# Pinning ScalarE's joinings, seeding an accumulator bank by a copy, and moving one residual update into the last block

## The chip, the cores and the metric

The kernel runs on one core of a Trainium2 chip. The core has TensorE (PE in the profile, with PEld for its weight loads), VectorE (DVE), ScalarE (ACT), GpSimd (POOL) and SyncE (SP), which issues most DMAs. The metric is the device time of one execution in microseconds (us).

## The reference, cut to what matters

One decoder layer on 256 tokens of width 2048, in float32: a half-step SwiGLU feed-forward network (FFN, inner width 5632), a mixer (input projection, a recurrent and a convolutional branch, output projection), a second FFN, and a final norm.

```
def swiglu_ffn(x, w_gate, w_up, w_down):
    return (jax.nn.silu(x @ w_gate) * (x @ w_up)) @ w_down
...
x = x + 0.5 * swiglu_ffn(rms_norm(x, ffn1_norm), w_gate1, w_up1, w_down1)
...                       # mixer: x = x + y @ w_out
x = x + 0.5 * swiglu_ffn(rms_norm(x, ffn2_norm), w_gate2, w_up2, w_down2)
return rms_norm(x, final_norm)
```

## The kernel before, in words

**Precision.** Every float32 operand of a product is split into a rounded part `hi` and a remainder `lo`, and a product is three matmuls (hi by hi, lo by hi, hi by lo). For the weights ScalarE makes `hi` by a copy (two halves of 128x1024 each, CAST in the profile), VectorE makes `lo` by a subtraction over 128x2048 (`parts_of`). A weight unit is 512 rows by 512 columns.

**The FFN.** Gate and up projections run column pair by column pair: `for s in range(5)`, each with one call of `seven` for gate and one for up; the first 512 columns are made ahead of this by `begin` or `begin_after`. After s = 0, 2 and 4 a call of `down` multiplies the hidden units made so far by `w_down`; it, too, has one `seven` in it. That makes 13 blocks per FFN and 26 in all.

**A block (`seven`).** Part of each block is a 2x2 block product done with seven products instead of eight (Winograd's form), the rest is usual products over further row units. It has four banks of PSUM, `a`, `c`, `e`, `d`. The order of PE's work is: product 0 into `a`; product 4 into `c`; usual product 0 into `e` and `c`; product 5 into `a`; usual 1 into `e` and `c`; product 6 into `a`; product 2 into `c`; usual 0 into `d` and `a`; product 3 into `a`; usual 1 into `a` and `d`; product 1 into `d`. A product is 12 matmuls, a usual product 24, so a block with two usual units is 180 matmuls. Between products VectorE forms combinations of weight units in place (`raw <- raw, raw`). Some partial sums are needed in more than one quadrant; `snap` has ScalarE copy a bank to a buffer in SBUF (`keep`, 13 buffers): `s1` is `a` after product 0, `s5` is `c` after product 4 (usual 0 can only go on accumulating into `c` once this copy is done), `u2` and `u3` later states of `a`. When a quadrant is complete, `done` adds the bank and its list of copies: quadrant (1, 1) is `e` with two copies, (0, 1) is `c` with one, (1, 0) is `a` alone, (0, 0) is `d` with `s1`. In gate and up `done` leads to `total` (VectorE additions), then Silu on ScalarE or the product of up and gate on VectorE; in `down` it leads to `update`, one VectorE operation on the residual `xres` for the bank and one for each copy.

**Turning the hidden tiles.** Each finished 128x512 hidden tile has to be transposed for use as a stationary operand. `part` shuffles its 16-bit halves apart on ScalarE (into a `plane`, two buffers) and issues a transposing DMA; `join` puts the halves together again on ScalarE (the joining, a COPY of 128x1024 16-bit values into a `plane`), and then splits the result into `hi` (ScalarE) and `lo` (VectorE), and where block sums of it are wanted copies it once more. `onward`, called after each multiply that has two targets, joins the tile that is on its way and parts the next. So a block of two usual units has four such points, and the four tiles that an up block leaves are turned during its own last two points and the next block's first three.

**Order.** A planner takes each engine's instructions in program order and may issue a later one ahead when, in its model, it is ready and the engine is free. The finished order is fixed: on the chip an engine works through its list and waits wherever an operand is late. `tc.keep_in_program_order(ins)` gives `ins` one constraint: it stands behind the instruction that was written just before it for the same engine. While `Engine.pinned` is true, every instruction of VectorE, ScalarE and TensorE gets it. Before, that holds in `begin` and from the last column's update at the end of the second FFN.

**The last `down`.** `side` holds banks for columns 0 and 3, which are multiplied directly: column 0 over all units first, then part of column 3, then the rest of column 0 and its `update` of the residual, then the block (columns 1 and 2), then the rest of column 3. In the last `down` `update` also calls `last`, which squares and sums the new residual on ScalarE (`junk_f`), and multiplies the residual by the final gain on VectorE; its first call loads that gain (`fin`) by a DMA issued on ScalarE's queue.

Of the kernel before, what the change touches and what calls it, by code (L numbers as in the profile page):

```python
# [12 lines left out]
U16 = mybir.dt.uint16  # L13
# [8 lines left out]
NT = S // P  # L22
# [27 lines left out]
def hybrid_block(ctx: ExitStack, tc: tile.TileContext, a: dict, out: bass.AP):  # L50
    nc = tc.nc
    Engine.pinned = False
    dve, act, pe = (Engine(tc, e) for e in (nc.vector, nc.scalar, nc.tensor))
# [29 lines left out]
    def bank(name):  # L83
        return psum.tile([P, 512], F32, tag="ps", name=name)

    def f32(ap):
        return ap.bitcast(F32)
# [62 lines left out]
    def big(name):  # L150

        return bigs.tile([P, UK, 2 * S], F32R, tag="big", name=name)
# [41 lines left out]
    def stationary(tile, t):  # L194

        return [(tile[:, j, t * P : (t + 1) * P], tile[:, j, S + t * P : S + (t + 1) * P]) for j in range(UK)]
# [148 lines left out]
    def quad(tile):  # L345
        return tile.rearrange("p (j c) -> p j c", j=UK)

    def seven(w, rows, cols, sf, xs, name, keep, done, between=None, ready=None):


        a, c, e, d = (bank(f"ps_{name}_{n}") for n in "aced")

        def get(u, n, kept=False):
            src = w[u * UK * P : (u + 1) * UK * P, cols[n] : cols[n] + CW]
            return load(src, f"{name}_{u}{n}", kept=kept)

        (r0, r1), two = rows, len(xs) > 1
        w11, first = ready or (get(r0, 0, True), None)
        w12 = get(r0, 1, True)
        b2, w22 = get(xs[0][0], 1), get(r1, 1)  # L360
        b3 = get(xs[1][0], 1) if two else None
        a2, w21 = get(xs[0][0], 0), get(r1, 0)
        a3 = get(xs[1][0], 0) if two else None

        def snap(ps, n):
            s = keep(f"{n}_{name}")
            act.copy(s, ps)
            return s

        def product_of(i, raw, ps, begin=False, end=True, blk=None):  # L370
            multiply([(ps, sf[i], begin, end)], blk or parts_of(raw, f"{name}_p{i}"), True)

        def usual(i, raw, n, *targets):

            blk = parts_of(raw, f"{name}_x{i}{n}")
            multiply([(ps, stationary(xs[i][1], t), b, z) for ps, t, b, z in targets], blk, True)

        product_of(0, w11, a, True, blk=first)
        s1 = snap(a, "s1")
        dve.tensor_tensor(w11, w12, w11, op=ALU.subtract)  # L380
        product_of(4, w11, c, True)
        s5 = snap(c, "s5")
        if between:
            between(0)
        usual(0, b2, 1, (e, 1, True, not two), (c, 0, False, False))
        if between:
            between(1)
        dve.tensor_tensor(w11, w22, w11, op=ALU.subtract)
        product_of(5, w11, a)
        u2 = snap(a, "u2")  # L390
        if between:
            between(2)
        if two:
            usual(1, b3, 1, (e, 1, False, True), (c, 0, False, False))
        dve.tensor_tensor(w12, w22, w12, op=ALU.subtract)
        product_of(6, w12, a)
        u3 = snap(a, "u3")
        done(1, 1, e, [u3, s5])
        product_of(2, w22, c)
        done(0, 1, c, [u2])  # L400
        usual(0, a2, 0, (d, 0, True, False), (a, 1, False, False))
        dve.tensor_tensor(w11, w21, w11, op=ALU.subtract)
        product_of(3, w11, a, end=not two)
        if two:
            usual(1, a3, 0, (a, 1, False, True), (d, 0, False, False))
        done(1, 0, a, [])
        product_of(1, w21, d)
        done(0, 0, d, [s1])

    def ffn(tag, norm, after, opening=False):  # L410
        with (
# [5 lines left out]
            wg, wu, wd = (a[f"ffn{tag}_w_{s}"][0] for s in ("gate", "up", "down"))  # L417
# [10 lines left out]
            mixed, flat = "p (f b) -> p b f", "p (b f) -> p b f"  # L428
# [10 lines left out]
            def join(two, u, t, h, again):  # L439
                if u not in hidden:  # L440
                    hidden[u] = big(f"h{tag}_{u}")
                act.copy(two.bitcast(U16).rearrange(mixed, b=2), h.bitcast(U16).rearrange(flat, b=2))
                two = quad(two)
                hi = hidden[u][:, :, t * P : (t + 1) * P]
                lo = hidden[u][:, :, S + t * P : S + (t + 1) * P]
                act.copy(hi, two)
                dve.tensor_tensor(lo, two, f32(hi), op=ALU.subtract)
                if again:
                    act.copy(quad(h), two)
                    turned[u, t] = quad(h)  # L450
# [13 lines left out]
            def on_the_way():  # L464
                return [*tiles, *(entry[0] for entry in moving)]
# [3 lines left out]
            units, vs, sf, ready = [], {}, {}, []  # L469
# [198 lines left out]
            xs = list(enumerate(units))[2:]  # L668
            turn_of["hold"] = False

            def down(last):
                us = sorted(set(hidden) | {tile[0] for tile in on_the_way()})
                others, (m, n) = us[:-2], us[-2:]
                end = last and tag == 2

                def update(c, t, *parts):
                    xr = xres[:, t, c * CW : (c + 1) * CW]
                    for p in parts:
                        dve.scalar_tensor_tensor(xr, p, 0.5, xr, op0=ALU.mult, op1=ALU.add)
                    if last:  # L680
                        after(c, t)

                side = {c: [bank(f"ps_d{tag}_{m}_{c}_{t}") for t in range(NT)] for c in (0, 3)}

                def add_units(c, units):
                    blks = [
                        (u, unit(wd[u * UK * P : (u + 1) * UK * P, c * CW : (c + 1) * CW], f"d{tag}_{m}_{c}_{u}"))
                        for u in units
                    ]
                    assert not {tile[0] for tile in on_the_way()} & set(units)  # L690
                    groups = [[0], [1]] if end and units == [n, m] else [[0, 1]]
                    for ts in groups:
                        for u, blk in blks:
                            multiply(
                                [(side[c][t], stationary(hidden[u], t), u == us[0], u == m) for t in ts], blk
                            )
                            pump(1.5 / len(groups))
                    if units[-1] == m:
                        Engine.pinned = end and c == 3
                        for t in range(NT):  # L700
                            update(c, t, side[c][t])

                sh, got, rest = {}, {}, []

                def block_sums():
                    return seven_of(
                        sh, hidden[m], hidden[n],
                        {(t, i): turned[u, t] for t in range(NT) for i, u in ((0, m), (1, n))},
                        quad(keep(f"hspare{tag}_{m}")),
                        [[quad(keep(f"hs{tag}_{m}_{i}_{z}", F32R)) for z in range(2)] for i in range(4)],  # L710
                    )

                def add(t, b, ps, tiles):
                    got[t, b] = [ps] + tiles
                    if (0, b) in got and (1, b) in got:
                        for i in range(NT):
                            update(2 - b, i, *got[i, b])

                for c, u in [(0, u) for u in others + [n]] + [(3, u) for u in others]:
                    add_units(c, [u])  # L720
                    if not on_the_way() and not rest:
                        rest.append(block_sums())
                add_units(0, [m])
                if tag == 1 and m == 5:
                    prepare()
                seven(
                    wd, (m, n), (2 * CW, CW), sh, [(u, hidden[u]) for u in others], f"d{tag}_{m}", keep, add,
                    lambda i: rest.pop()() if rest else None,
                )
                for units in [[n, m]] if end else [[n], [m]]:  # L730
                    add_units(3, units)
                hidden.clear()
                turned.clear()

            for s in range(5):
                cs = (CW + 2 * s * CW, 2 * CW + 2 * s * CW)
# [20 lines left out]
                    if s == 0 and not opening and i != 1:  # L757
                        (sums, lambda: normalise(3))[i // 2]()

                seven(wg, (0, 1), cs, sf, xs, f"g{tag}_{s}", keep, gate, meanwhile, ready.pop() if ready else None)  # L760
                seven(wu, (0, 1), cs, sf, xs, f"u{tag}_{s}", keep, up)
                if s % 2 == 0:
                    down(s == 4)
            extra.clear()
# [45 lines left out]
    with tc.tile_pool(name="mixer", bufs=1) as mp, tc.tile_pool(name="mixw", bufs=2) as mw:  # L810
# [197 lines left out]
        for c in range(NC_D):  # L1008
            cs = slice(c * CW, (c + 1) * CW)
# [96 lines left out]
```

## Time and profile before

| | |
|---|---|
| median of three runs (lowest, highest) | 1740.79 us (1740.5, 1741.35) |
| the profiled execution's own time | 1740.98 us |
| its span, first to last instruction | 1739.2 us |
| mean granted TensorE clock | 0.997 |
| busy: PE, weight loads, DVE, ACT | 1709.3, 1416.1, 1485.4, 1135.1 us |

Nearly all instructions pass through one helper, so their line is 43 and groups are told apart by tile names: `ps_g_a` is bank `a` of a gate block (`u` for up, `d` for down), `hi_g_p` and `lo_g_p` are the parts of a weight unit or combination used in one of the seven products, `hi_g_x` those of a usual product, `plane` the turning buffer. Names like `s_g`, `u_g`, `z`, `s_u` are buffers of `keep` and go on being called by the name under which the tile was made. In a table of windows the number behind x is the count of instructions. The times of matmuls are modelled as pipelined, so a busy PE does not mean a PE at its full rate; counts of matmuls per window show that better.

### The profile page before, as it was taken

How to read it: one execution, taken by the hardware profiler on the slowest of the kernel's cores; microseconds unless marked ns; L12 is line 12 of the kernel's file. 1: busy time of each engine (PE TensorE's matmuls, PEld its weight loads, DVE VectorE, ACT ScalarE, POOL GpSimd, SP SyncE). 2: the span in 40 equal slices, each digit the busy share in tenths (PEclk: the TensorE clock that was granted, in tenths of full speed). 3: DMA queues.
4: the chain of work that ended last, by engine and by line, in shares of the span. 5: the costliest groups of instructions: out<-in, count | busy, mean ns of one | idle time of the engine just before them, and what ended most of it. 6: DMA issues, size and time to landing. Idle time of an engine off the chain costs nothing. (4 is left out here: it accounts for less than half of the span.)

```text
span 1739.2 us, 20156 instructions
## 1 busy us (share of the span) xinstructions
PE 1709.3 (98%) x7859; PEld 1416.1 (81%) x7859; DVE 1485.4 (85%) x1233; ACT 1135.1 (65%) x1433; POOL 6.9 (0%) x32
## 2 busy tenths in 40 slices
PE   8999999999999999999999999999999999999998
PEld 6888787888887888888888888787787888887876
DVE  7997998989899888687986669989799888889786
ACT  6767567676567676665665456675567765676854
POOL 1000000000000000000000000000000000000000
PEclk9999999999999999999999999999999999999999
DMA  8666567594567585556556564595476656576843
GB/s 297 201 218 184 203 215 211 191 303 163 183 217 221 204 247 169 189 172 193 173 194 209 203 217 133 195 289 174 167 235 221 214 173 219 194 212 206 277 167 106
DMA packets 220383, 354.75 MB, mean 204 GB/s; under 512 B 52100, under 2 KB 54528, under 8 KB 220160
## 3 DMA queue, kind: packets, MB, share of 16 engines
q1 hardware_dynamic: 219824, 352.36, 62.5%
q8 instruction: 61, 1.00, 0.2%
q10 hardware_dynamic: 144, 1.05, 0.2%
q14 instruction: 34, 0.28, 0.0%
q0 software_dynamic: 320, 0.07, 0.0%
HBM read 339.82 MB, written 2.10 MB: 197 GB/s over the span
## 5 line engine op out<-in xcount | busy, mean ns | idle before, releaser
L43 DVE TENSOR_TENSOR lo_u_p<-raw_u,hi_u_p 128x2048 fp32r<-128x2048 f32 x70 | 159.2, 2287 | 19.5 <-ACT hi_u_p L43 19.0
L43 DVE TENSOR_TENSOR lo_g_p<-raw_g,hi_g_p 128x2048 fp32r<-128x2048 f32 x66 | 150.1, 2287 | 29.8 <-ACT hi_g_p L43 29.7
L43 ACT CAST hi_u_p<-raw_u 128x1024 fp32r<-128x1024 f32 x140 | 141.1, 1047 | 52.2 <-DVE raw_u L43 23.0
L43 ACT CAST hi_g_p<-raw_g 128x1024 fp32r<-128x1024 f32 x132 | 132.2, 1046 | 55.9 <-DVE raw_g L43 35.7
L43 PE MATMUL ps_d<-hi_d,h 128*128 128x512 f32 x704 | 167.2, 389 | 0.0
L43 PEld LDWEIGHTS ps_d<-hi_d,h 128*128 128x128 f32 x704 | 132.1, 188 | 27.4
L43 PE MATMUL ps_in<-xT_nm,hi_in 128*128 128x512 f32 x640 | 153.8, 391 | 0.0
L43 PEld LDWEIGHTS ps_in<-xT_nm,hi_in 128*128 128x128 f32 x640 | 117.2, 188 | 22.9 <-ACT tha L43 0.4
L43 ACT CAST hi_d_p<-raw_d 128x1024 fp32r<-128x1024 f32 x84 | 85.4, 1047 | 74.0 <-DVE raw_d L43 37.1
L43 DVE TENSOR_TENSOR lo_d<-raw_d,hi_d 128x2048 fp32r<-128x2048 f32 x44 | 100.6, 2288 | 30.1 <-ACT hi_d L43 28.1
L43 ACT CAST hi_in<-raw_in 128x1024 fp32r<-128x1024 f32 x80 | 80.0, 1045 | 65.8 <-PE ps_in L43 45.6
L43 DVE TENSOR_TENSOR lo_in<-raw_in,hi_in 128x2048 fp32r<-128x2048 f32 x40 | 91.3, 2285 | 35.1 <-ACT hi_in L43 34.8
L43 DVE TENSOR_TENSOR lo_d_p<-raw_d,hi_d_p 128x2048 fp32r<-128x2048 f32 x42 | 95.8, 2285 | 15.8 <-ACT hi_d_p L43 14.5
L43 ACT CAST hi_u_x<-raw_u 128x1024 fp32r<-128x1024 f32 x80 | 80.4, 1047 | 42.8 <-PE ps_u_c L43 19.6
L43 DVE TENSOR_TENSOR raw_u<-raw_u,raw_u 128x2048 f32<-128x2048 f32 x40 | 91.6, 2290 | 12.1 <-DMA raw_u<-in_ffn_w_up_dram 11.5
L43 ACT CAST hi_d<-raw_d 128x1024 fp32r<-128x1024 f32 x88 | 88.7, 1045 | 19.1 <-PE ps_d_d L43 7.6
L43 DVE TENSOR_TENSOR lo_g_x<-raw_g,hi_g_x 128x2048 fp32r<-128x2048 f32 x40 | 91.5, 2286 | 6.9 <-ACT hi_g_x L43 6.8
L43 ACT CAST hi_g_x<-raw_g 128x1024 fp32r<-128x1024 f32 x80 | 80.4, 1044 | 22.2 <-PE ps_g_c L43 10.6
L43 DVE TENSOR_TENSOR lo_u_x<-raw_u,hi_u_x 128x2048 fp32r<-128x2048 f32 x40 | 91.4, 2284 | 0.2 <-ACT hi_u_x L43 0.2
L43 DVE TENSOR_TENSOR raw_g<-raw_g,raw_g 128x2048 f32<-128x2048 f32 x37 | 84.5, 2285 | 4.8 <-DMA raw_g<-in_ffn_w_gate_dram 4.6
L43 PE MATMUL ps_d<-lo_d,h 128*128 128x512 f32 x352 | 87.3, 389 | 0.0
L43 PEld LDWEIGHTS ps_in<-xT_nm,lo_in 128*128 128x128 f32 x640 | 82.2, 191 | 3.2
(387 smaller groups left out, 3661.7 us busy)
## 6 DMA issues: line engine op xcount, KB each, us to landing
raw_d<-in_ffn_w_down_dram SPq DMA_DIRECT2D x88, 1024.0 KB, 5.3
raw_u<-in_ffn_w_up_dram SPq DMA_DIRECT2D x87, 1024.0 KB, 5.3
raw_g<-in_ffn_w_gate_dram SPq DMA_DIRECT2D x86, 1024.0 KB, 5.4
raw_in<-in_w_in_dram SPq DMA_DIRECT2D x40, 1024.0 KB, 5.1
raw_o<-in_w_out_dram SPq DMA_DIRECT2D x16, 1024.0 KB, 5.1
xres<-in_x_dram SPq DMA_DIRECT2D x4, 512.0 KB, 7.5
raw_u<-in_ffn_w_up_dram SPq DMA_DIRECT2D x2, 512.0 KB, 9.3
raw_g_first<-in_ffn_w_gate_dram SPq DMA_DIRECT2D x1, 1024.0 KB, 11.9
```

Source lines behind the costliest of these rows:

```text
L43: ins = getattr(self.engine, name)(*args, **kwargs)
```

## The change

Three edits.

1. In `join` the first ScalarE copy is put through `tc.keep_in_program_order`.
2. `seven` gets a parameter `whole`, true unless told otherwise. Where it is true, ScalarE copies bank `a` after product 0 into bank `d` instead of into an SBUF buffer, usual 0 accumulates on that bank from its first matmul on, and quadrant (0, 0) is `d` alone. It is false for gate and up of s = 0 in both FFNs and for gate of s = 3 in the first, so it is true in 21 of the 26 blocks: 7 gate, 8 up, 6 down.
3. In the last `down` the update of column 0 (with `last`) is written inside the block, after its first usual product, instead of ahead of the block. `Engine.pinned` is set as before from column 3 on.

```
-        s1 = snap(a, "s1")
+        s1 = None if whole else snap(a, "s1")
+        if whole:
+            act.copy(d, a)
...
-        usual(0, a2, 0, (d, 0, True, False), (a, 1, False, False))
+        usual(0, a2, 0, (d, 0, not whole, False), (a, 1, False, False))
...
-        done(0, 0, d, [s1])
+        done(0, 0, d, [] if whole else [s1])
...
-                act.copy(two.bitcast(U16).rearrange(mixed, b=2), h.bitcast(U16).rearrange(flat, b=2))
+                tc.keep_in_program_order(
+                    act.copy(two.bitcast(U16).rearrange(mixed, b=2), h.bitcast(U16).rearrange(flat, b=2))
+                )
...
-                    if units[-1] == m:
-                        Engine.pinned = end and c == 3
+                    if units[-1] == m and not (end and c == 0):
+                        Engine.pinned = end
                         for t in range(NT):
                             update(c, t, side[c][t])
...
+                def within(i):
+                    if i == 0:
+                        rest.pop()()
+                    elif i == 1 and end:
+                        for t in range(NT):
+                            update(0, t, side[0][t])
...
-                    lambda i: rest.pop()() if rest else None,
+                    within,
...
+                      s > 0 and (tag, s) != (1, 3))
-                seven(wu, (0, 1), cs, sf, xs, f"u{tag}_{s}", keep, up)
+                seven(wu, (0, 1), cs, sf, xs, f"u{tag}_{s}", keep, up, whole=s > 0)
```

More of the change, by code (lines that the diff above doesn't have):

```diff
@@ L346, in quad, with seven @@
         return tile.rearrange("p (j c) -> p j c", j=UK)
-    def seven(w, rows, cols, sf, xs, name, keep, done, between=None, ready=None):
+    def seven(w, rows, cols, sf, xs, name, keep, done, between=None, ready=None, whole=True):
         a, c, e, d = (bank(f"ps_{name}_{n}") for n in "aced")
@@ L758, in meanwhile @@
                         (sums, lambda: normalise(3))[i // 2]()
-                seven(wg, (0, 1), cs, sf, xs, f"g{tag}_{s}", keep, gate, meanwhile, ready.pop() if ready else None)
-                seven(wu, (0, 1), cs, sf, xs, f"u{tag}_{s}", keep, up)
+                seven(wg, (0, 1), cs, sf, xs, f"g{tag}_{s}", keep, gate, meanwhile, ready.pop() if ready else None,
+                      s > 0 and (tag, s) != (1, 3))
+                seven(wu, (0, 1), cs, sf, xs, f"u{tag}_{s}", keep, up, whole=s > 0)
                 if s % 2 == 0:
```

## The prediction

> **What bounds the kernel now.** I read the page's head first, then the table of windows, then the list of waits.
>
> ```profile
> span 1739.2 us, 20156 instructions
> PE 1709.3 (98%) x7859; PEld 1416.1 (81%) x7859; DVE 1485.4 (85%) x1233; ACT 1135.1 (65%) x1433; POOL 6.9 (0%) x32
> ```
>
> PE is the bound over the whole span. The change takes no matmul away, so it can only win back places where PE waits. How much there is shows in counts per window: first a dense stretch, then the four places where an up block of s = 1 or 3 is followed by the next gate block, then the start of the last block of the kernel.
>
> ```profile
> 300.00:400.00 100.00, 100.00 (x442) 82.42 (x441) 86.51 (x56) 68.80 (x79) 0.00 (x0) 1.00 0.72 235
> 290.00:312.00 22.00, 21.16 (x90) 16.18 (x89) 21.41 (x13) 17.63 (x21) 0.00 (x0) 1.00 0.56 174
> 541.00:563.00 22.00, 20.61 (x87) 15.68 (x87) 20.85 (x13) 17.50 (x21) 0.00 (x0) 1.00 0.60 182
> 1311.00:1333.00 22.00, 20.84 (x89) 15.98 (x88) 21.16 (x12) 16.28 (x19) 0.00 (x0) 1.00 0.65 202
> 1561.00:1583.00 22.00, 20.51 (x88) 15.62 (x87) 20.76 (x13) 17.45 (x21) 0.00 (x0) 1.00 0.58 183
> 1674.00:1693.00 19.00, 16.65 (x67) 13.28 (x66) 17.54 (x13) 12.56 (x19) 0.00 (x0) 0.91 0.32 110
> ```
>
> The columns are the window, its length, and busy time with count of PE, PEld, DVE, ACT and POOL, then the granted clock. The dense rate is 100 us / 442 = 0.226 us a matmul. A window of 22 us holds 97.3 at that rate; the four hold 90 + 87 + 89 + 88 = 354 of 389, so 35 are missing, 35 x 0.226 = 7.9 us. The last row holds 67 of 84: 17 x 0.226 = 3.8 us. Together 11.7 us, 0.7% of the span, is what the edits can reach. In the four windows VectorE is busy for 21 of 22 us, so it has no reserve there either.
>
> What makes the four places late is in the chain of work through the third of them (start, length, what; some rows left out):
>
> ```profile
> 1297.47 6.64 DMA u_g<-plane
> 1304.13 1.37 ACT plane L43
> ...
> 1314.05 1.90 ACT hi_g_x L43 x2
> 1315.95 0.49 ACT s_g L43
> 1316.48 2.12 PE ps_g_c L43 x8
> ```
>
> A transposing DMA lands at 1304.1, a joining waits for it, and from there ScalarE's list runs late up to its copy `s5` (1315.95), for which PE stands still. The timeline of the same place gives the durations:
>
> ```profile
> 1304.13 1.36 ACT L43 COPY plane<-u_g 128x1024 uint16<-128x1024 uint16 x1 [2.35 <-DMA u_g<-plane]
> 1305.53 0.62 ACT L43 CAST h<-plane 128x512 fp32r<-128x512 f32 x1
> 1306.91 0.68 DVE L43 TENSOR_TENSOR h<-plane,h 128x512 fp32r<-128x512 f32 x1
> 1307.51 0.68 DVE L43 TENSOR_TENSOR s_u<-ps_u_d,s_u 128x512 f32<-128x512 f32 x1
> 1309.85 1.04 ACT L43 CAST hi_g_x<-raw_g 128x1024 fp32r<-128x1024 f32 x1
> 1310.80 0.58 ACT L43 COPY s_g<-ps_g_a 128x512 f32<-128x512 f32 x1
> 1313.24 0.76 PEld L43 LDWEIGHTS ps_g_c<-lo_g_p,xs 128*128 128x128 f32 x4 [0.51 <-DVE lo_g_p L43]
> 1315.45 0.30 PEld L43 LDWEIGHTS ps_g_e<-lo_g_x,x 128*128 128x128 f32 x2 [1.21 <-DVE lo_g_x L43]
> 1316.48 1.69 PEld L43 LDWEIGHTS ps_g_c<-hi_g_x,x 128*128 128x128 f32 x8 [0.73 <-ACT s_g L43]
> ```
>
> PE is held three times within 3.3 us: twice by VectorE (the remainders `lo_g_p` and `lo_g_x`), once by ScalarE. In the whole-run list of waits the four places are the four waits on `lo_g_x`:
>
> ```profile
> ACT plane L43 <- DMA u_g<-plane: 13.0, 7, 2.7
> PEld ps_g_e L43 <- DVE lo_g_x L43: 4.8, 4, 1.2
> ```
>
> **Part 1, the joinings.** Which joinings does the pin move? By program order the four tiles of an up block are joined behind the last usual product of that block and behind the first three usual products of the next. The first (before this stretch) stands behind casts that are over by then and stays. The second (1304.13) must now stand behind both `hi_g_x` casts of the next block's first usual product, the later of which starts at 1309.85, so it moves by about 1309.85 + 1.04 - 1304.13 = 6.8 us. Its DMA has landed by then, so the wait of 2.35 us is gone, and 1.36 + 0.62 of ScalarE's work and 0.68 of VectorE's (`h<-plane,h`, 1306.91) leave the stretch before `s5`. The third and fourth move behind later casts in the same way. Nothing needs these tiles before the next `down`, one block and a half later (a block is 180 x 0.226 = 41 us). The joinings inside `down` already stand behind the casts they would be pinned to, so they keep their waits; PE does not wait on them now. The transposing DMA and `part` are not pinned; a moved joining holds its `plane` longer, so the third tile's `part` may come later, with the same time to spare.
>
> **Part 2, the first product into `d`.** Removed: one VectorE operation of 0.68 us in 21 blocks, 14.3 us of 1485.4. ScalarE's copy stays; its destination is another. A copy from bank to bank is not in this trace: it could cost somewhat less than the 0.58 us of the copy to SBUF or more, up to a cast of the same size from SBUF, 0.62. I take 0.58, the nearest row, since source, shape and type are the same; 21 x 0.04 = 0.8 us on an engine with 35% idle is nothing either way. New waits: the copy needs bank `d` free some 22 us earlier in the block (the banks of a block were last used two blocks before, a whole block of 41 us ago, or by column 3 and the last block's quadrants, which are read while 48 matmuls, 10.9 us, of column 3 run), and PE's first matmul on `d` needs the copy, about 20 us after it. Both at nothing. On PE's path the removed addition counts only where VectorE is late, at the four places (`s_u<-ps_u_d,s_u` at 1307.51, right ahead of the late remainders). Elsewhere VectorE is hidden behind PE.
>
> Together at each of the four places VectorE has 0.68 + 0.68 = 1.36 us less ahead of `lo_g_x`; PE's two waits on it are 0.51 and 1.21 as the weight loads show them, of which some 0.2 each is the gap that PE's pipeline has anyway. So VectorE's lateness is about covered. ScalarE has 2.35 + 1.36 + 0.62 = 4.3 us less ahead of `s5`, which was late by 0.73. What is late next is VectorE again, with some tenths in hand. I take back three quarters: 0.75 x 7.9 = 5.9 us. Bounds: nothing (VectorE stays late) and 7.9.
>
> **Part 3, column 0's residual.** The chain through the start of the last block, and its timeline:
>
> ```profile
> 1684.28 3.08 PE ps_d_c L43 x8
> 1687.37 1.52 PE ps_d_e L43 x4
> 1688.89 0.92 PE ps_d_c L43 x4
> ```
>
> ```profile
> 1679.10 0.63 ACT L43 ACTIVATE junk_f<-xres 128x512 f32<-128x512 f32 x1 [3.48 <-DVE xres L43]
> 1679.64 0.19 ACT L43 ACTIVATION_READ_ACCUMULATOR junk_f<-xres 128x1 f32 x1
> 1681.30 0.56 ACT L43 COPY s_d<-ps_d_a 128x512 f32<-128x512 f32 x1
> 1681.78 1.28 DVE L43 SCALAR_TENSOR_TENSOR xres<-xres,fin 128x512 f32<-128x512 f32 x2
> 1683.65 0.58 ACT L43 COPY s_d<-ps_d_c 128x512 f32<-128x512 f32 x1
> 1684.28 3.08 PE L43 MATMUL ps_d_c<-hi_d_x,h 128*128 128x512 f32 x8 [2.35 <-ACT s_d L43]
> ```
>
> ScalarE idles 3.48 us for the new residual, then does two squares with their reads, 2 x (0.63 + 0.19) = 1.6 us, then `s1`, casts, and `s5` at 1683.65, for which PE waits 2.35 us. Moved behind usual 0, the squares come after `s5`; `s1` can be copied in the idle time, so `s5` comes 1.6 + 0.56 = 2.2 us earlier, and 0.2 of the stall stays. The granted clock of this window is 0.91: the 12 matmuls from 1684.28 to 1688.89 take 4.61 us where the dense rate gives 2.71, so 1.9 of the 3.8 us is a slow stretch of PE straight after its stall. Without the stall I take it to go as well. The moved work is two updates and two gain products (4 x 0.64 us on VectorE) and the squares; it now competes with the block's remainders, but what follows in order, `u2`, has a usual product of 24 x 0.226 = 5.4 us of PE's work between it and its use. The load of the gain is issued with the first update, so by its new place its bytes could come later:
>
> ```profile
> 1650.62 0.37 ACTq L1035 DMA_DIRECT2D fin<-in_final_norm_dram  x1
> 1656.16 0.43 DVE L43 TENSOR_SCALAR fin<-fin 128x512 f32<-128x512 f32 x1 [1.57 <-DMA fin<-in_final_norm_dram]
> ```
>
> It was issued some 20 us ahead of its written place, so it already runs when ScalarE's queue has room, and I count it at nothing; if issued only at the block's usual 0, VectorE would wait up to 1656.16 - 1650.62 = 5.5 us for it. I take 3.8 - 0.3 = 3.5 us. Bounds: -1.7 (a wait of 5.5 less the 3.8 that goes) and 3.8.
>
> [...]
>
> **Sum.** 5.9 + 3.5 = 9.4 us off the profiled execution's 1740.98, which is its span of 1739.2 and 1.8 around it: 1731.6. The median of the three runs shown is 0.2 lower, so 1731.4; I say 1731.5. 0.2%, 3.5 us, is about what a measurement of this kernel can tell from no change.
>
> **The rivals.** (a) VectorE stays the limit at the four places. For it speaks that it is busy 21 of 22 us there. If only the 0.68 of the addition comes off, because the planner puts another VectorE operation into the room of the joining's, it is 4 x 0.68 = 2.7 us, with 3.5 from the end 6.2: 1734.6. Against it: by the pin the joining's operation cannot stand there.
>
> [...]
>
> (c) Slower. A pinned joining stands between casts and `s5` of a gate block and waits there for its DMA. The longest such wait now is this one, in the last `down`, where nothing of PE's hung on it:
>
> ```profile
> 1657.25 1.35 ACT L43 COPY plane<-s_g 128x1024 uint16<-128x1024 uint16 x1 [5.07 <-DMA s_g<-plane]
> ```
>
> Behind a late joining stand `u2`, `u3` and the casts of the coming product. PE can go on for about one usual product's second half, 8 x 0.226 = 1.8 us. With the third and fourth joining of four places each waiting 5.07 us, PE loses 8 x (5.07 - 1.8) = 26 us; less the 9.4 that is 1757. It decides from a wait of 1.8 + 9.4 / 8 = 3.0 us at each. Against it: the pin spaces the four points at 24 or 36 matmuls, 5.4 to 8.1 us, and the turn above took 6.64 from issue to landing, so a joining that is written a point after its `part` finds most of its DMA done.
>
> (d) Nothing: the planner's list changes in places that the edits do not name, and stalls move. There are such places of 1 to 3 us in the table of this sort now, which no edit touches, as at 1226 and 160:
>
> ```profile
> 1226.00:1242.00 16.00, 14.11 (x61) 10.71 (x60) 12.14 (x7) 8.82 (x11) 0.00 (x0) 1.00 0.22 67
> 160.00:182.00 22.00, 19.90 (x84) 15.07 (x83) 21.93 (x16) 15.80 (x19) 0.00 (x0) 1.00 0.30 97
> ```
>
> They lack 10 and 13 matmuls, 2.3 and 2.9 us. Four new ones of that size eat the gain: 1740.
>
> **How the numbers follow.** My forecast (a gain of 7 to 11.7 us) 0.45; (a) and (b) together (3.5 to 7) 0.28; (d) 0.10, of which 0.06 lies within 3.5 us of no change and 0.04 beyond it on the slower side; (c) 0.12 slower, 0.05 for a gain above 11.7 because VectorE's 14.3 us helps at places like 160. Faster by over 0.2%: 0.45 + 0.28 + 0.05 = 0.78; same 0.06; slower 0.16. The range goes from 1727, the whole 11.7 and 2 more, to 1743, which takes in (a), (b) and most of (d) and leaves out (c). The forecast's own range is 1729 to 1734.
>
> **What would show it.** In the profile after: the four windows of 22 us hold 94 or more matmuls each; the waits of joinings on the DMA of `u_g` fall from 13.0 us to under 6; the list has no wait of PE on `lo_g_x` over 0.5 us; VectorE's busy time is about 14 us lower and it has 21 operations fewer, ScalarE's count is the same; the last block's first 19 us hold 82 or more, with the clock at 1. The prediction fails if stalls of the size of the old ones stand in other gate blocks, if joinings wait there, or if `xres` operations wait for `fin` in the last block.

## The result, and the profile after

| | before | after |
|---|---|---|
| median of the runs taken side by side (lowest, highest) | 1741.35 us (1737.88, 1744.51) | 1734.17 us (1731.66, 1735.56) |
| ratio after / before, 95% interval | | 0.9956 [0.9944, 0.9968] |
| the profiled execution's own time, its span | 1740.98, 1739.2 us | 1735.05, 1733.1 us |

The change makes the kernel 0.44% faster, 7.7 us by the ratio (5.6 to 9.7), where 9.4 were forecast; 1734.17 us is inside the range of 1727 to 1743 and just above the forecast's own 1729 to 1734. The head of the page after, busy time and count by engine:

```profile
span 1733.1 us, 20143 instructions
PE 1708.6 (99%) x7859; PEld 1417.9 (82%) x7859; DVE 1472.5 (85%) x1212; ACT 1136.4 (66%) x1433; POOL 6.9 (0%) x32
```

VectorE has 21 operations fewer and is 12.9 us less busy, ScalarE's count is unchanged. The table of windows after, with the same stretches as before and one more (window, length, busy time and count of PE, PEld, DVE, ACT, POOL, granted clock, DMA share, GB/s):

```profile
290.00:312.00 22.00, 21.63 (x94) 17.04 (x93) 21.76 (x13) 20.50 (x24) 0.00 (x0) 1.00 0.57 175
541.00:563.00 22.00, 21.63 (x95) 17.08 (x94) 21.82 (x13) 20.37 (x24) 0.00 (x0) 1.00 0.63 202
1311.00:1333.00 22.00, 21.05 (x92) 16.78 (x91) 21.95 (x15) 19.14 (x22) 0.00 (x0) 1.00 0.66 206
1561.00:1583.00 22.00, 21.63 (x95) 17.11 (x94) 21.84 (x14) 19.70 (x23) 0.00 (x0) 1.00 0.65 202
1674.00:1693.00 19.00, 19.00 (x86) 15.73 (x85) 17.74 (x14) 14.06 (x20) 0.00 (x0) 1.00 0.55 180
160.00:182.00 22.00, 19.95 (x78) 15.04 (x77) 21.97 (x15) 14.89 (x18) 0.00 (x0) 0.93 0.31 99
```

The four places at which an up block meets the next gate block hold 94, 95, 92 and 95 matmuls, 22 more than before; 13 of 389 are still missing. The last block's start is full, with the clock at 1. But the stretch of the first `down` at 160 now holds 78 instead of 84, at a clock of 0.93. The prediction took this stretch and the one at 1226 for places that no edit touches; part 2 touches both, by a copy into bank `d` at 165.99 and at 1225.48.

To follow single places through many kernels I added up what PE loses at each: for every matmul of 512 columns the time from its start to the next start, less the 0.227 us that the dense run needs (differences under 0.03 us left out; other sizes likewise against their own median). All kernels have the same 7859 matmuls, and a place means the same matmuls in each. The places are called by their time in the kernel before. In us, from one profiled execution each, with all kernels of the next section. Such an execution can be one of the longer ones of its kernel: that of `col0_only`, 1746.76 us, is the longest of twelve, that of `pin_copy_down`, 1740.02 us, the longest of six.

```
                       four places  last block  166-182   1230   1430    660   whole run
before                     8.51        4.22       3.19    2.44   0.83   0.00     29.5
after                      3.93        0.00       4.74    1.75   2.01   0.74     23.8
pin_only                   1.64        4.43       3.02    2.44   0.00   0.33     23.3
copy_only                 12.66        0.00       3.51    1.76   1.30   0.58     30.8
col0_only                 10.69        4.80       4.87    2.87   0.87   0.00     35.8
col0_all                   3.83        0.00       3.25    3.28   3.37   0.00     24.8
no_col0                    3.54        0.00       2.88    2.59   3.04   0.77     22.9
no_copy                    1.64        1.64       2.76    2.44   0.00   0.00     18.9
pin_copy_last              1.64        0.00       4.20    2.44   0.00   0.00     19.2
pin_copy_last_pad          1.64        0.00       4.44    2.44   0.00   0.00     18.7
pin_swap                   4.44        0.00       1.07    3.20   1.76   0.00     23.3
pin_copy_up                1.64        0.00       5.43    2.44   0.00   0.00     24.5
pin_copy_down              4.49        6.66       5.14    2.44   0.00   0.00     29.2
pin_copy_last_col0         1.64        0.00       2.81    2.44   0.00   0.00     19.0
```

So the gain of the profiled execution, 5.9 us, is 4.6 from the four places and 4.2 from the last block, less 1.6 at 166-182, 1.2 at 1430 and 0.7 at 660, and 0.7 more at 1230. What PE waits for at 1430, a place in a `down` where the loss has grown, the timeline after tells (start, length, engine, what, then idle time ahead of it and its releaser):

```profile
1413.74 2.00 ACT L43 CAST hi_d_p<-raw_d 128x1024 fp32r<-128x1024 f32 x2 [6.89 <-DMA raw_d<-in_ffn_w_down_dram]
...
1418.10 4.62 DVE L43 TENSOR_TENSOR raw_d<-raw_d,raw_d 128x2048 f32<-128x2048 f32 x2
...
1422.18 1.98 PE L43 MATMUL ps_d_a<-hi_d_p,h 128*128 128x512 f32 x8
...
1431.34 1.89 PE L43 MATMUL ps_d_c<-hi_d_x,h 128*128 128x512 f32 x7 [1.74 <-ACT s_d L43]
```

### The profile page after: what moved, and what is told of

Its sections match the earlier page's. It is cut to its first block, busy times and chain, and to the rows that moved or that the text cites. A ratio compares the mean times of both kernels' runs of the same rounds, so it can differ in the third digit from the quotient of the medians.

```text
span 1733.1 us, 20143 instructions
## 1 busy us (share of the span) xinstructions
PE 1708.6 (99%) x7859; PEld 1417.9 (82%) x7859; DVE 1472.5 (85%) x1212; ACT 1136.4 (66%) x1433; POOL 6.9 (0%) x32
## 5 line engine op out<-in xcount | busy, mean ns | idle before, releaser
L43 DVE TENSOR_TENSOR raw_u<-raw_u,raw_u 128x2048 f32<-128x2048 f32 x40 | 91.6, 2290 | 13.5 <-DMA raw_u<-in_ffn_w_up_dram 12.9
```

The lines of the kernel that those rows point to most:

```text
L43: ins = getattr(self.engine, name)(*args, **kwargs)
```

## The experiments

The kernels differ from the kernel after by a few switches. "No copy" puts `whole = False` at the head of `seven`; "no pin" takes `tc.keep_in_program_order` off the joining; "no column 0" writes column 0's residual ahead of the last block again:

```diff
 # no copy: first line of seven
+        whole = False
 # no pin
-                tc.keep_in_program_order(
                     act.copy(two.bitcast(U16).rearrange(mixed, b=2), h.bitcast(U16).rearrange(flat, b=2))
-                )
 # no column 0
-                    if units[-1] == m and not (end and c == 0):
-                        Engine.pinned = end
+                    if units[-1] == m:
+                        Engine.pinned = end and c == 3
...
-                    elif i == 1 and end:
+                    elif i == 1 and False:
```

The runs were taken in three sets: the first heading below, the second, and the last two together. Each set stands against its own runs of the kernel before, with medians of 1742.97, 1740.47 and 1743.22 us, so kernels of different sets are compared by their ratios.

### Each part alone, and column 0 inside every down

`pin_only` is no copy and no column 0.

> Only the joinings are pinned. Theory A (ScalarE's wait for the transposing DMA sets the four places between an up block and the next gate block): the pin alone brings most of what the four places gave, 3.5 to 5 us less than the kernel before, and the four windows of 22 us hold 93 or more matmuls each against 87 to 90. Theory B (VectorE is full there, so its removed addition counts): the pin alone brings 0 to 2 us and the windows stay at 91 or less, with PE's waits on lo_g_x still in the list. In both the last block's first 19 us keep about 67 matmuls.

Measured: 1735.03 us, ratio 0.9952 [0.9935, 0.9969]: the pin alone gives what the whole change gives. Its windows at the same four places and at the last block:

```profile
288.00:310.00 22.00, 21.86 (x97) 17.75 (x96) 22.00 (x13) 20.70 (x24) 0.00 (x0) 1.00 0.57 161
538.00:560.00 22.00, 21.86 (x97) 17.75 (x96) 22.00 (x15) 19.96 (x23) 0.00 (x0) 1.00 0.56 177
1307.00:1329.00 22.00, 21.86 (x97) 17.79 (x96) 22.00 (x16) 19.23 (x22) 0.00 (x0) 1.00 0.61 187
1556.00:1578.00 22.00, 21.86 (x96) 17.75 (x96) 22.00 (x14) 18.45 (x22) 0.00 (x0) 1.00 0.63 199
1672.00:1691.00 19.00, 16.45 (x66) 13.12 (x65) 16.40 (x13) 13.54 (x20) 0.00 (x0) 0.91 0.49 166
```

The four places are full, better than with the whole change, as theory A had it; the last block is as late as before. By the ratio it is 8.4 us, more than the 3.5 to 5 that were expected.

`copy_only` is no pin and no column 0.

> Only the first product's copy into bank d, in the same 21 blocks. Theory A: 0 to 1.5 us less than before, and ScalarE goes on waiting for the joinings' DMA as before (u_g 13 us in all). Theory B: 3 us or more less, since 0.68 us of VectorE goes at each of the four places and another in each of 17 other blocks. Both: the bank-to-bank copy takes 0.56 to 0.60 us, and VectorE has 21 operations fewer.

Measured: 1740.23 us, 0.9982 [0.9969, 0.9995]. The copy helps nothing at the four places (12.7 us lost), and the joinings' waits on `u_g` rise to 23.8 us. By the ratio the kernel is still 3.1 us faster (0.9 to 5.4), as much as theory B asked, but not for its reason: the stall of the last block is gone, although both of the residual's squares still stand ahead of `s5`:

```profile
1681.71 0.64 ACT L43 ACTIVATE junk_f<-xres 128x512 f32<-128x512 f32 x1 [1.21 <-DVE xres L43]
...
1683.29 0.63 ACT L43 ACTIVATE junk_f<-xres 128x512 f32<-128x512 f32 x1
...
1686.31 0.58 ACT L43 COPY s_d<-ps_d_c 128x512 f32<-128x512 f32 x1
...
1687.32 1.98 PE L43 MATMUL ps_d_c<-hi_d_x,h 128*128 128x512 f32 x8
```

`col0_only` is no pin and no copy.

> Only column 0's residual inside the last block. Theory C (the squares ahead of s5 made the stall): the 2.35 us wait on s5 in the last block is gone, 2.0 to 4.2 us less than before; the upper end if the slow stretch of PE goes with the stall, the lower end if it turns up at another stall. Rival D (the last block's gain in the changed kernel came from the planner's other order, not from the residual's place): under 1 us.

Measured: 1740.26 us, 0.9985 [0.9972, 0.9998]. The stall stays, with one square (`junk_f`) ahead of `s5` now; the other follows it at 1690.44:

```profile
1687.88 0.63 ACT L43 ACTIVATE junk_f<-xres 128x512 f32<-128x512 f32 x1 [0.25 <-DVE xres L43]
...
1689.44 0.57 ACT L43 COPY s_d<-ps_d_c 128x512 f32<-128x512 f32 x1
...
1690.07 2.58 PE L43 MATMUL ps_d_c<-hi_d_x,h 128*128 128x512 f32 x8 [2.94 <-ACT s_d L43]
```

So the two squares ahead of `s5` are not enough for the stall, and with one of them moved it stays. By the ratio this kernel is 2.6 us faster (0.3 to 4.9), the size that theory C asked of the stall's end; since the stall is still there, the gain does not come from its end, and its source was not found.

`col0_all` is the kernel after with `elif i == 1:` and no `end` in the two conditions, so that column 0 is updated inside the block in all six downs.

> The changed kernel, with column 0's residual inside the block in all six downs instead of the last alone. If the stalls on s5 at 660 and 1429 us of the changed kernel (0.7 and 2.0 us) have the cause that the last block's had, they go, and it is 1.5 to 3 us faster than the changed kernel, 8.5 to 10 less than before. If they come from PE running into VectorE's chain through the block's combinations (raw_d, hi_d_p), which are late for their own reason, it is within 1 us of the changed kernel.

Measured: 1734.5 us, 0.9952 [0.9933, 0.9971], not to be told from after. The stall at 1430 is still there (3.4 us lost; without column 0's move, below, 3.0), so it does not come from column 0's place. That at 660 is gone.

### Two parts together, and the copy in one block

`no_col0` is the kernel after without its third part.

> The changed kernel with column 0's residual back ahead of the last block (joinings pinned, first product copied into d). Theory E: the stall at the start of the last block hangs on the last hidden tile: its last VectorE operation came late, so its turn and joining came late, ScalarE waited some 5 us for that DMA, and VectorE ran late from there to the block. The copy into d takes one of the two operations away. Then the stall stays away without the residual's move, and the time is within 1.5 us of the changed kernel. Theory C (the residual's squares): the stall comes back, 2 to 4 us slower than the changed kernel.

Measured: 1734.2 us, 0.9968 [0.9956, 0.9981]: as after, within the intervals. The end stall is away without the residual's move.

`no_copy` has the pin and column 0 inside.

> The changed kernel without the copy into d (joinings pinned, column 0's residual inside the last block). Theory E: the stall of 2 to 3 us at the last block's start is there, behind a joining that waits 4 to 5 us, and the four places between up and gate lose 0.4 us each as with the pin alone; within 1.5 us of the pin alone. Theory C: the stall is gone, and it is 2 to 4 us faster than the pin alone.

Measured: 1731.01 us, 0.9947 [0.9934, 0.996]. The four places are as with the pin alone, and 1.6 us of the end's loss stay: PE waits 1.37 us at `s5`, less than the 2 to 3 of theory E and not nothing as theory C had it.

`pin_copy_last` has the pin, no column 0, and the copy in a single block, the last up block, in front of the last `down` (`whole` is false by default and in the gate call):

```diff
-                seven(wu, (0, 1), cs, sf, xs, f"u{tag}_{s}", keep, up, whole=s > 0)
+                seven(wu, (0, 1), cs, sf, xs, f"u{tag}_{s}", keep, up, whole=(tag, s) == (2, 4))
```

> Joinings pinned, and the copy into d in one block alone of the 26, the last up block of the second FFN; one VectorE operation fewer than with the pin alone. Theory E: the stall at the last block's start (4.4 us with the slow stretch, with the pin alone) goes, and it is 2 to 4.5 us faster than the pin alone, 1730.5 to 1733 against 1735. Rival F (the copy helps by the sum of VectorE's 21 operations): no difference from the pin alone that can be measured, 0.7 us at most.

Measured: 1728.96 us, 0.9938 [0.9926, 0.995], the lowest median of its set. One block's copy takes the whole end stall away. In that block (0, 0) needs no addition of `s1`, so its hidden tile is finished one VectorE operation earlier. To see whether that operation matters, `pin_copy_last_pad` adds a buffer of zeros there instead:

```diff
             act.copy(d, a)
+            s1 = keep(f"pad_{name}")
+            nc.gpsimd.memset(s1, 0.0)
...
-        done(0, 0, d, [] if whole else [s1])
+        done(0, 0, d, [s1])
```

> As the kernel with the copy in the last up block alone, but quadrant (0, 0) there gets back its addition of a buffer, which holds zeros: the copy into d stays and VectorE has as many operations as with the pin alone. Theory E: the stall of 2 to 4.4 us is back, with a joining that waits 4 us or more ahead of it. If the copy into d helps in another way (an earlier bank, another order of PE), the stall stays away.

Measured: 1730.48 us, 0.9944 [0.9932, 0.9956]; the end stall is still gone. So it is not the operation saved either, and theory E falls. What the kernels with and without the stall have apart is the order in which ScalarE turns the last two tiles in front of the last `down`. With the pin alone (`part` takes 1.04 us, a joining 1.36; the last tile is `s_g`):

```profile
1641.91 1.37 ACT L43 COPY plane<-z 128x1024 uint16<-128x1024 uint16 x1 [1.03 <-DMA z<-plane]
...
1643.13 1.05 ACT L43 COPY plane<-s_g 128x1024 uint16<-128x1024 uint16 x1
...
1650.63 1.35 ACT L43 COPY plane<-s_g 128x1024 uint16<-128x1024 uint16 x1 [3.95 <-DMA s_g<-plane]
...
1662.70 4.62 DVE L43 TENSOR_TENSOR raw_d<-raw_d,raw_d 128x2048 f32<-128x2048 f32 x2
...
1667.69 1.98 PE L43 MATMUL ps_d_a<-hi_d_p,h 128*128 128x512 f32 x8
```

With the copy in that block:

```profile
1638.73 1.05 ACT L43 COPY plane<-s_g 128x1024 uint16<-128x1024 uint16 x1 [0.17 <-DVE s_g L43]
...
1642.10 1.36 ACT L43 COPY plane<-z 128x1024 uint16<-128x1024 uint16 x1 [0.42 <-DMA z<-plane]
...
1643.33 1.35 ACT L43 COPY plane<-s_g 128x1024 uint16<-128x1024 uint16 x1
...
1659.58 4.62 DVE L43 TENSOR_TENSOR raw_d<-raw_d,raw_d 128x2048 f32<-128x2048 f32 x2
...
1667.72 1.98 PE L43 MATMUL ps_d_a<-hi_d_p,h 128*128 128x512 f32 x8
```

In the first, the last tile's `part` stands behind the third tile's joining. Its transposing DMA starts late, the last joining waits 3.95 us for it, ScalarE's casts of the down weights stand behind that joining, and VectorE starts its pair of combinations (4.62 us) 1667.69 - 1662.70 = 5.0 us ahead of product 0. In the second, `part` is ahead of the joining, the last joining waits for nothing, and the pair starts 8.1 us ahead. The same order divides all 14 kernels: the last tile's `part` stands behind the third tile's joining in the five with the stall (before, `pin_only`, `col0_only`, `no_copy`, `pin_copy_down`) and ahead of it in the nine without.

### The order alone

`pin_swap` is `pin_only` with `onward` parting the next tile before it joins the moving one; no copy anywhere:

```diff
-                if moving:
-                    tile, two = moving.popleft()
-                    join(two, *tile)
+                turned = moving.popleft() if moving else None
                 if tiles:
                     tile = tiles.popleft()
                     moving.append((tile, part(*tile)))
+                if turned:
+                    tile, two = turned
+                    join(two, *tile)
```

> Only the joinings are pinned (no copy into the last quadrant's bank, column 0's residual ahead of the block), and at each point of the turn the next tile's part is written ahead of the moving tile's joining, where it stood behind it. Theory O (the stall at the start of the last block comes from the last tile's part standing behind the third tile's joining; its order decides, not VectorE's removed addition): the last joining of the last down waits under 1 us (3.95 with the joinings pinned alone), ScalarE's s5 of the last block holds PE for under 0.5 us (2.7), and the time is some 3 to 4 us under that of the pin alone, about 1729 to 1732. Theory E (fewer VectorE operations decide): the wait of 4 us or the stall of 2.7 us stays, about 1735.

Measured: 1732.25 us, 0.994 [0.9927, 0.9952]. The last block in its timeline:

```profile
1643.70 1.04 ACT L43 COPY plane<-s_g 128x1024 uint16<-128x1024 uint16 x1
...
1644.90 1.38 ACT L43 COPY plane<-z 128x1024 uint16<-128x1024 uint16 x1 [0.16 <-DMA z<-plane]
...
1649.07 1.38 ACT L43 COPY plane<-s_g 128x1024 uint16<-128x1024 uint16 x1
...
1664.07 4.62 DVE L43 TENSOR_TENSOR raw_d<-raw_d,raw_d 128x2048 f32<-128x2048 f32 x2
...
1672.20 1.98 PE L43 MATMUL ps_d_a<-hi_d_p,h 128*128 128x512 f32 x8
...
1679.46 1.98 PE L43 MATMUL ps_d_c<-hi_d_x,h 128*128 128x512 f32 x8
```

The joining does not wait, the lead is 8.1 us, and PE does not stand still: the order alone removes the end stall. And without a single copy the swap brings what the copies brought elsewhere: 1.1 us lost at each of the four places (0.41 with the pin alone, 0.83 to 1.33 after) and a stall at 1430 of 1.5 us. So by the ratios, 0.994 and 0.9952, the time is not to be told from that of the pin alone; the 3 to 4 us that were expected came at the end, not in the sum.

Whether PE stands still at `s5` hangs on that lead and on the squares ahead of `s5`. From the pair's start to product 0's, and PE's wait at `s5`:

```
                            lead    wait    sum
last block, two squares ahead of s5
  before                    5.20    2.35    7.55
  pin_only                  4.99    2.55    7.54
  pin_copy_down             4.01    3.59    7.60
  copy_only, pin_swap       8.14, 8.13   none
last block, one square ahead of s5
  col0_only                 3.81    2.94    6.75
  no_copy                   5.40    1.37    6.77
  after                     8.14    none
block at 1430 (no squares)
  before                    5.25    0.56    5.81
  after                     4.08    1.74    5.82
  no_col0                   3.05    2.78    5.83
  pin_swap                  4.32    1.49    5.81
  pin_only, pin_copy_up     7.97, 6.92   none
```

VectorE's pair needs a start 7.55 us ahead of product 0 where two squares are on ScalarE's list, 6.76 with one, 5.8 with none. So where the lead is short a square with its read is worth 0.8 us, by the two groups of the last block, and about 1 us by an estimate from two different blocks, 6.76 - 5.8; where the lead is 8.1 us it is worth nothing.

### Where the copies bring the other stalls

The last runs ask which blocks' copies bring the stalls at 1430 and 660, and whether part 3 helps the best kernel. `pin_copy_up` has `whole` true in the up blocks of s = 2 and 4 alone, `pin_copy_down` in the downs alone.

> Joinings pinned; the first product is copied into the last quadrant's bank in the up blocks of s = 2 and 4 of both FFNs only, that is in the blocks straight ahead of a down with a full wait for its tiles. Theory U (the stalls at 660 and 1429 come with the copy in the up block ahead of the down, through its last tiles' order): a stall of 0.6 us or more at one of these places at least, about 1730 to 1732. Theory D (they come with the copy inside a down): neither, end stall away, about 1729.

> Joinings pinned; the first product is copied into the last quadrant's bank in the downs' blocks only. Theory D: the stalls at 660 (0.7 us) and 1429 (2 to 3 us) are there; theory U: neither is. By both, the stall at the start of the last block stays (2.7 us), since the last up block is as it was; the four places lose about 0.4 us each. 1733 to 1738.

Measured: `pin_copy_up` 1733.17 us, 0.9941 [0.9927, 0.9955]; `pin_copy_down` 1735.42 us, 0.9958 [0.9943, 0.9972]. Neither has a stall at 1430 or 660, so both theories fall as put. That leaves the gate blocks, the other up blocks, or a combination of them; which was not tried. In part theory U is borne out all the same: in `pin_copy_up` the cast ahead of the place at 1430 does wait for its load, 4.66 us at 1413.42, but the lead stays at 6.92 us, which is enough. `pin_copy_up` loses 0.8 to 1.6 us inside up blocks that it touches (at 336, 585 and 1354) instead, and `pin_copy_down` keeps the end stall, as both theories had it. What neither had: at the third of the four places `pin_copy_down` loses 3.3 us instead of 0.4, in blocks that have no copy.

`pin_copy_last_col0` adds part 3 to `pin_copy_last`.

> Joinings pinned, the copy in the last up block alone, and column 0's residual inside the last block. If the residual's place has no price of its own once PE does not stand still at the block's start: as without it, 1728 to 1731, and no wait of PE over 0.5 us in the last 60 us. If it brings VectorE late in the block: 0.5 to 1.5 us more.

Measured: 1731.34 us, 0.9933 [0.992, 0.9947]. No wait of PE in the last block, and by the ratios no difference from the kernel without it: where the lead suffices the residual's place is worth nothing.

## Why the prediction was right, and where not

**The sum.** 9.4 us were forecast, 7.7 measured. The places named gave 4.6 + 4.2 = 8.8 us in the profiled executions, near the forecast, and stalls that moved to places not named took 2.8 of it back: rival (d) came in part. Yet these are not places that no edit touches: those at 160, 660, 1230 and 1430 all lie in blocks that get part 2's copy. The single terms were not the forecast's, 4.6 against 5.9 and 4.2 against 3.5, and the second came by another way than the one named; that the sum came out near is in part luck.

**Part 1 held, and was undersized.** The pin moved the second joining from 1304.13 to 1310.58 behind the casts, where it waits for nothing. Part 2's copy between banks took 0.58 us, the value assumed:

```profile
1310.07 0.58 ACT L43 COPY ps_g_d<-ps_g_a 128x512 f32<-128x512 f32 x1
...
1310.58 1.33 ACT L43 COPY plane<-u_g 128x1024 uint16<-128x1024 uint16 x1
```

Alone it took back 8.51 - 1.64 = 6.9 us of 8.5 where parts 1 and 2 together were to take back 5.9 of 7.9. Rival (c) did not come: no pinned joining of a gate block waits for its DMA.

**Part 2 failed at "on PE's path the removed addition counts only where VectorE is late, at the four places".** There it costs. With it 3.93 us are lost, without it 1.64. The waits on `lo_g_x` are gone as forecast, but VectorE stays the limit there, as rival (a) had it in kind: of the weight loads' waits on VectorE, that on `lo_g_p` is longest now. And the joinings' wait on `u_g`, 13.0 us before, is not under 6:

```profile
ACT plane L43 <- DMA u_g<-plane: 10.9, 7, 2.6
...
PEld ps_g_c L43 <- DVE lo_g_p L43: 3.9, 5, 1.4
```

The reason is order again, and at three of the places it is PE's own. At the second, first after, where product 0 starts at 538.17, then the pin alone, where it starts at 536.39:

```profile
541.12 2.28 DVE L43 TENSOR_TENSOR lo_g_p<-raw_g,hi_g_p 128x2048 fp32r<-128x2048 f32 x1
...
542.70 0.39 PE L43 MATMUL ps_g_e<-hi_g_x,x 128*128 128x512 f32 x1
...
543.46 1.20 PE L43 MATMUL ps_g_c<-lo_g_p,xs 128*128 128x512 f32 x4 [0.37 <-DVE lo_g_p L43]
```

```profile
539.34 2.28 DVE L43 TENSOR_TENSOR lo_g_p<-raw_g,hi_g_p 128x2048 fp32r<-128x2048 f32 x1
...
540.92 0.61 PE L43 MATMUL ps_g_e<-hi_g_x,x 128*128 128x512 f32 x2
...
541.67 1.20 PE L43 MATMUL ps_g_c<-lo_g_p,xs 128*128 128x512 f32 x4
```

VectorE begins `lo_g_p` 2.95 us behind product 0's start in both. But in front of the wait for it PE's list holds one matmul of usual 0 after, and two with the pin alone, so PE stands still for 0.53 us instead of 0.30, and it loses some 0.2 us more at product 5. The first and the fourth place are alike. At the third, where 1.33 us are lost against 0.41, VectorE begins `lo_g_p` 3.54 us behind product 0's start: an earlier cast on ScalarE's list waits for a load, and with the pin alone it does not (there it starts at 1287.68):

```profile
1292.34 2.00 ACT L43 CAST hi_u_x<-raw_u 128x1024 fp32r<-128x1024 f32 x2 [3.08 <-DMA raw_u<-in_ffn_w_up_dram]
```

That the copies cost here is shown by `no_copy`; how they do it is read from the traces, and no run moved these matmuls or that load by themselves. `pin_swap`, with 1.1 us lost at each place, has another order than these two: its second joining (1305.04) stands ahead of the casts `hi_g_x`.

The seven waits of joinings on `u_g` lie elsewhere now: at the four places, where they made 2.05 + 2.59 + 2.35 + 2.69 = 9.7 of the 13.0 us, there is none, and those left are at the ends of up blocks in front of a `down`, the longest, 2.62 us, at 369.98. The prediction had said that joinings inside `down` keep their waits. They did not: the waits on `z` and `s_g` there were ten, 17.2 us in all, and are three, 3.6 us.

**Part 3 had the size and not the cause.** Its step by which both squares come after `s5`, and `s5` 2.2 us earlier, did not hold: in the last block after, one square (1677.20) still goes ahead of `s5` (1678.77), and only the other (1679.76) follows it. With the lead of 8.14 us that this kernel has, the move is worth nothing, as `no_col0` shows; where the lead is short, one square moved is worth 0.8 us. The mechanism was not without ground: with no square ahead of `s5` the kernel before, by its lead of 5.20 us and the 5.8 of the block at 1430, would have waited some 0.6 us instead of 2.35, an estimate across two blocks. The 4.2 us of the last block came from part 2, through the order of the last tile's turn, at a place where the prediction had said of the joining's 5.07 us that "nothing of PE's hung on it". It hung on it by a chain of 24 us: late `part`, late DMA, waiting joining, late casts, late pair of combinations, late `s5`. That wait stood in the list and its price was not followed behind the joining.

**The stall at 1430.** The prediction had no term for it, though the block is one of those that part 2 edits. Its lead is short because ScalarE's cast waits 6.89 us for a load of down weights (the row of 1413.74 above). The issues on SyncE's queue show why the load is late, after and with the pin alone:

```profile
1392.36 4.08 SPq L436 DMA_TRANSPOSE z<-plane  x2
1396.53 14.80 SPq L168 DMA_DIRECT2D raw_d<-in_ffn_w_down_dram  x5
```

```profile
1388.73 1.24 SPq L437 DMA_TRANSPOSE z<-plane  x1
1390.11 3.21 SPq L168 DMA_DIRECT2D raw_d<-in_ffn_w_down_dram  x2
1394.95 1.24 SPq L437 DMA_TRANSPOSE s_g<-plane  x1
1396.29 10.58 SPq L168 DMA_DIRECT2D raw_d<-in_ffn_w_down_dram  x3
```

With two parts in a row, two transposes stand ahead of five loads; with the pin alone two of the five go out between the transposes, 6.4 us earlier by the clock and 3.8 us earlier counted from product 0. This is read from the traces; no run moved the loads by themselves, and the order on the queue is not enough: `pin_copy_up` has both transposes ahead of the five loads, too, and does not stall. The cause of the smaller stall at 660 stays open.

**The slow stretch.** "Without the stall I take it to go as well", which rested on one window, the only one in its table with a clock under 1 (0.91), was half right: the stretch left the last block, and after it stands at 179, in the window at 160 above (clock 0.93). It follows a stall of 1.9 us there, where before it followed one of 2.5 (2.35 by the timeline). So in this execution the 1.9 us counted for it were not won for the whole run. The chances have a part for (b), little gain at the end; the profile after does not show that: of the 4.22 us lost in the last block nothing is left, and no `xres` operation waits for `fin`.

**What would show it** held for VectorE's and ScalarE's counts, the last block (86 matmuls, at least 82 were asked), the waits on `lo_g_x`, and three of the four windows (92 in the third); it failed for the waits on `u_g`.

## What to carry to other kernels

A wait on an engine that is not the bound has to be followed down that engine's own list: what stands behind it, and who needs that 20 us later. Where a planner makes the order, an edit that saves an operation can matter only by the order that it tips, and the same tip can help one place and cost at others; so make the parts of a change separately, and apply each only to the blocks where it pays (here the pin everywhere and the copy in one block, 1728.96 us, against the pin and all 21 copies, 1734.2 us in the same set; part 3 added nothing to either).

## What the runs showed of the hardware

A stretch in which each matmul of 512 columns takes 0.43 us instead of 0.227, mostly 7 to 9 of them, 1.4 to 1.9 us in all, comes behind the first 15 us of the run in 8 of the 14 kernels' profiled executions, and not always at the same place. In the kernel with column 0's move alone it comes three times, two of them in these windows:

```profile
174.00:184.00 10.00, 8.11 (x27) 5.84 (x27) 10.00 (x8) 7.14 (x9) 0.00 (x0) 0.83 0.55 180
1570.00:1578.00 8.00, 6.99 (x24) 5.25 (x24) 6.42 (x4) 7.17 (x8) 0.00 (x0) 0.79 0.86 256
```

Every such stretch begins 3 to 5 us after PE began to stand still, and a stall of 1.9 us can have one behind it: that at 175 after, with 0.45 just ahead of it. But the same stall at 175 has none in the kernel before and in `pin_only`, that of 1.5 to 1.9 us at 1190 never has, and 2.9 and 3.3 us at 1430 in `no_col0` and `col0_all` have none; at the last block stalls of 2.5 us and more had one in all four kernels, and that of 1.5 us in `no_copy` had none. So each of these stretches had a stall ahead of it, but not each stall had such a stretch behind it, and what decides was not found. The stretches fit the 3 to 10 us by which the runs of one kernel differ: the eleven runs of the kernel before in the last set go from 1739.65 us at a mean granted clock of 0.999 to 1749.41 us at 0.994. So a difference of 2 us between two of these kernels is not settled by their medians.
